# The weight and input streams of a convolutional feed-forward block are issued in another order, and the last block ends in two column halves

## The chip, the cores and the metric

One NeuronCore of a Trainium2 chip runs the whole program. The metric is the device time of one execution in microseconds. The kernel before takes 2106.96 us (median of 3 runs, 2106.72 to 2106.99).

## The reference, cut to what matters

One layer of a hybrid decoder trunk on 2048 positions and 1024 channels, float32. All of the work around the change is in the second half of the layer:

```python
x = x + concat([hm, hp]) @ w_out                 # output projection, residual
h = rmsnorm(x, g_ffn)
up = causal_dwconv(h @ w_up, w_ffn_conv) + b_ffn_conv   # 2 x 2816 channels, width 3
gate, val = up[..., :D_FF], up[..., D_FF:]
x = x + (silu(gate) * val) @ w_down
return rmsnorm(x, final_norm)
```

## The kernel before

Every float32 product is made of three matmuls. An operand is split into a rounded high part (`split_h`, L94, a cast on ACT) and the low part that is left (`split_l`, L100, a subtraction on DVE), and `products` (L112 to L114) issues high x high, high x low and low x high into one PSUM bank.

Positions come in four blocks of 512 (`b`). After the mixer, `out_proj` (L908) multiplies by `w_out` and adds the residual; its evacuation (L948) adds a PSUM bank to an `xr` tile that SP has loaded, ACT stores the sum to DRAM (`x2d`) and squares it (L919), and DVE adds the squares up (`ss`, L925). A bank is free for the next group when its square has been added up.

The feed-forward part runs in the order up half 0, down 0, down 1, up half 1, down 2, down 3. An up half handles two blocks at once by a scheme with seven products instead of eight, for each of 22 column blocks `j` (`PRODUCTS`: 11, S1, S2, 12, S3, 22, S4, where S1 to S4 take sums and differences of input quarters and of weight quarters). One product group (`j`, `p`) is 12 matmuls of 512 columns. Groups that build on another's result in the same bank have to wait until ACT has copied that bank to an `r` tile (`copied`, L1296): S2 after 11, S3 after S2, 22 after S3. `up_order` says in which order the groups run.

The order of the work is written out by hand. The main program issues matmuls, and after every few of them calls `tick()`, which lets each side stream (a generator) issue its next step. `until` lets a stream skip ticks until a flag is set, and `need` ticks until it is. Each engine then runs its own instructions in the order in which they were issued. The side streams that matter here:

- `w_stream` (L1051): for each weight item, in one tick the sum or difference of quarters on DVE if the product wants one (`w_source`, L1033) and the rounding on ACT, in the next tick the low part on DVE. There are nine slots for finished items. `raw_load` (L1020) loads a unit of weights on SP's queue when the unit before the last is used up.
- `b_first` (L1106): the 28 inputs (7 products x 4 row blocks) of the first up half. `scaled` multiplies each of the 16 loaded tiles by a vector on ACT (L1098) and by the inverse root on GpSimd (L1099), one tile to a tick; the main part of `b_first`, one tick behind, subtracts where the product wants it (L1102) and rounds; the low part follows one tick later. It starts in the middle of the last `out_proj` (`at`, L1225), which first issues two weight loads of 1 MB on SP, then the `xr` loads.
- `activate` (L1258): convolution taps (L1266 on ACT, L1269 on DVE), Silu (L1276, ACT), product (L1278, DVE) and store of one column block.
- `last_scale` (L1250): the inverse root for the last block, from inside the first up half.
- `squares2` and `final` (L1398, L1418): squares of the down part's results, the final RMSNorm and the stores.

`down(b)` (L1357) runs two halves of four PSUM banks; each weight item is one row block of 128 by 512 columns. All four banks of a half finish together, at the last row block.

Of the kernel before, what the change touches and what calls it, by code (L numbers as in the profile page):

```python
# [6 lines left out]
F32 = mybir.dt.float32  # L7
# [76 lines left out]
def trunk(tc, x, xT, w_in, w_gate, w_pool, w_out, w_up, w_down, vecs, cst, out):  # L84
# [43 lines left out]
    with ExitStack() as ctx:  # L128
# [136 lines left out]
        def until(*flag):  # L265
            while flag not in flags:
                yield
# [711 lines left out]
        PRODUCTS = ("11", "S1", "S2", "12", "S3", "22", "S4")  # L979
        A11, S1, S2, A12, S3, A22, S4 = range(7)  # L980
        NS, NS1, NW, NW1, NX = 28, 14, 9, 6, 5
        HOLD = NS1 - 6
        SLOTS = [f"mixT{i}" for i in range(KT)] + [f"s{i}" for i in range(HOLD)] + [f"hT{i}" for i in range(6)] \
            + [f"s{HOLD + i}" for i in (2, 3, 0, 1, 4, 5)]
# [16 lines left out]
        for j in range(NJ):  # L1001
            if j + 1 < NJ:
                up_order += [(j + 1, A11), (j, A22), (j + 1, S1), (j, S4), (j + 1, S2), (j + 1, A12), (j + 1, S3)]
            else:
                up_order += [(j, A22), (j, S4)]
        items, raw_units, first_item = [], [], {}
        for part in ("u0", "d0", "d1", "u1", "d2", "d3"):
            first_item[part] = len(items)
            n = int(part[1])
            if part[0] == "u":  # L1010
                items += [("u", n, j, p) for j, p in up_order]
                raw_units += [("u", n, j) for j in range(NJ)]
            else:
                items += [("d", n, h, j) for h in range(2) for j in range(NJ)]
                raw_units += [("d", n, h, i) for h in range(2) for i in range(0, NJ, 4)]
# [16 lines left out]

        def w_source(it, raw):  # L1033

            if it[0] == "d":
# [4 lines left out]
            if p == S1:  # L1040
                src = state["s1"] = ff1.tile([P, 512], F32, tag="sum", name="sum")
                dve.tensor_tensor(out=src, in0=q[1][0], in1=q[1][1], op=ALU.add)  # L1042
                return src
            if p == S2:
                dve.tensor_tensor(out=q[1][0], in0=q[0][0], in1=q[1][0], op=ALU.subtract)
                dve.tensor_tensor(out=q[0][0], in0=state.pop("s1"), in1=q[0][0], op=ALU.subtract)
            elif p == S4:
                dve.tensor_tensor(out=q[0][1], in0=q[0][1], in1=q[0][0], op=ALU.subtract)
            return {A11: q[0][0], S2: q[0][0], A12: q[0][1], S3: q[1][0], A22: q[1][1], S4: q[0][1]}[p]

        def w_stream():  # L1051

            for n, it in enumerate(items):
                while n >= NW and n - NW not in w_used:
                    yield
                if n == NW1 - 1:
                    yield from until("rr")
                elif NW1 <= n < NW1 + 2:
                    yield from until("op", NB - 1)
                elif n == NW1 + 2:  # L1060
                    yield from until("ff2")
                u = ("u", *it[1:3]) if it[0] == "u" else ("d", *it[1:3], it[3] // 4 * 4)
                while u not in raw_tiles:
                    yield
                src = w_source(it, raw_tiles[u])
                w = w_slot(n)
                split_h(w[:, 0], src)
                yield
                split_l(w[:, 0], w[:, 1], src)
                ws[n] = w  # L1070
                del w, src
                flags.add(("w", n))
                if it[3] == S4 if it[0] == "u" else it[3] % 4 == 3 or it[3] == NJ - 1:
                    del raw_tiles[u]
                    raw_load(raw_at[u] + 2)

        def x_tile():
            return ff1.tile([P, 512], F32, tag="x", name="x", bufs=NX)
# [27 lines left out]
        def b_first():  # L1106
# [27 lines left out]
            load(1)  # L1134
            yield from wait(2)
            sides.add(scaled())
            for p in range(7):
                for kk in range(4):
                    if p < 4:
                        yield from until("x2", p, kk)  # L1140
                    if p == S1:
                        sub(x[0, kk], x[1, kk], x[0, kk])
                    elif p == S2:
                        sub(x[1, kk], x[2, kk], x[1, kk], pool)
                        sub(x[0, kk], x[2, kk], x[0, kk])
                    elif p == A22 and kk == 0:
                        for i in range(4):
                            sub(x[3, i], x[3, i], x.pop((0, i)))
                    i = {A11: 0, S1: 0, S2: 0, A12: 3, S3: 1, A22: 3, S4: 2}[p]
                    yield from b_put(0, p, kk, x.pop((i, kk)) if p > A12 else x[i, kk])  # L1150

        def b_prep(hh):

# [71 lines left out]
        def at(hf):  # L1225
            nonlocal ff1
            if hf == 0:
                need("pool", NB - 1)
                need("ho", NB - 1)
                ph1.release()  # L1230
                sm1.release()
                ff1 = tc.alloc_tile_pool(name="ff1", bufs=1, side="right", reuse_waits="tile")
                raw_load(0)
                raw_load(1)
                sides.add(s_stream())
                sides.add(w_stream())

# [20 lines left out]
        def activate(hh, j, pre):  # L1258

            if hh and j < 2:  # L1260
                yield from until("fin", 1)
            y = [q_tile(4 + 2 * gv + j % 2)[:, 0:HT] for gv in range(2)]
            for gv in range(2):
                ch = gv * NJ + j
# [12 lines left out]
            flags.add(("act", hh, j))  # L1277
            dve.tensor_tensor(out=y[0], in0=y[0], in1=y[1], op=ALU.mult)  # L1278
            yield from wait(2)
            sp.dma_start(act_d[hh][j], y[0].rearrange("p (a c) -> p a c", a=2))  # L1280
# [76 lines left out]
        def down(b):  # L1357
# [10 lines left out]
                flags.add(("acc", b))  # L1368
            sides.add(acc_load())
            for h in range(2):  # L1370
                o = []
                for _ in range(4):
                    o.append(nbank([P, BT]) if len(down_banks) % 6 in (2, 3) else big())
                    down_banks.append(0)
                for j in range(NJ):
# [3 lines left out]
                    for i in range(4):  # L1379
# [15 lines left out]
                        if i % 2:  # L1395
                            tick()

        def squares2(b, acc, k, x):  # L1398

            if k == 0:  # L1400
# [12 lines left out]
                give(slot)  # L1413
            flags.add(("sq", b, k))
            if k == KT - 1:
                sides.add(final(b, acc))

        def final(b, acc):  # L1418

            last = b == NB - 1  # L1420
# [4 lines left out]
            yield from spread_rsqrt(r, f(ones_r), [state.pop("ss")], (0, 1, 0, 1) if last else (8, 2, 0, 1))  # L1425
            flags.add(("summed", b))
            for k in range(KT):
                x, g = acc[k // 2][:, k % 2], vec[:, V_FIN + k:V_FIN + k + 1]
                if last and k in (1, 3, 5):
                    act.activation(x, x, AF.Copy, scale=g)  # L1430
                    pool.tensor_tensor(out=x, in0=x, in1=r, op=ALU.mult)
                else:
                    dve.scalar_tensor_tensor(out=x, in0=x, scalar=g, in1=r, op0=ALU.mult, op1=ALU.mult)  # L1433
                if k % 2:
                    sp.dma_start(out[k // 2][:, :, b * BT:(b + 1) * BT], acc[k // 2])
                if not last and k % 2:
                    yield
                yield
            flags.add(("fin", b))
# [63 lines left out]
```

## Time and profile before

| | |
|---|---|
| median of 3 runs | 2106.96 us |
| the profiled execution | 2107.88 us, its span 2106.2 us |
| TensorE busy, matmuls | 1997.9 us (95%), 8876 |
| VectorE (DVE) | 1449.0 us (69%) |
| ScalarE (ACT) | 1043.5 us (50%) |
| GpSimd (POOL) | 182.7 us (9%) |
| granted TensorE clock, mean | 0.977 |

Busy shares are means over the whole span. The stages differ: TensorE is busy all the time in the down parts, and the other engines leave it waiting in a few places between and inside the other stages.

### The profile page before, as it was taken

The numbers are of one execution on the slowest core, as the hardware profiler recorded it, in microseconds if no ns is written. First come the engines' busy times: TensorE is split into PE (matmuls) and PEld (weight loads), VectorE is DVE, ScalarE is ACT, GpSimd is POOL, SyncE is SP. The second block draws the span as 40 slices with busy tenths as digits, with TensorE's granted clock in tenths as the row PEclk, the third lists the DMA queues.
The fourth block names the chain that finished last, engine by engine and source line by source line (L and its number), as shares of the span: only waits on it lengthen the run. The fifth ranks groups of instructions, "written<-read, shape, count | busy, mean of one in ns | idle before, by whom it ended". The sixth has DMA issues, their size and how long they took to land. (4 is left out here: it accounts for less than half of the span.)

```text
span 2106.2 us, 24399 instructions
## 1 busy us (share of the span) xinstructions
PE 1997.9 (95%) x8876; PEld 1627.0 (77%) x8876; DVE 1449.0 (69%) x2320; ACT 1043.5 (50%) x1838; POOL 182.7 (9%) x263
## 2 busy tenths in 40 slices
PE   8999999998997599999998999989999999999996
PEld 6777877776885488788886888877888888788885
DVE  6587777776675677777778546577777777765433
ACT  5655655755644444545446444344444544544321
POOL 1003002011021400000000001120000000000000
PEclk9999999999999799999999999999999999999998
DMA  5433544442347112222224644432212221375431
GB/s 188 148 106 114 158 144 135 131 155 71 109 147 249 55 66 95 89 77 80 90 80 153 228 150 180 142 108 96 105 71 80 91 90 71 125 245 190 143 117 40
DMA packets 107384, 258.62 MB, mean 123 GB/s; under 512 B 9472, under 2 KB 14080, under 8 KB 107264
## 3 DMA queue, kind: packets, MB, share of 16 engines
q1 hardware_dynamic: 101936, 247.37, 34.6%
q10 hardware_dynamic: 5328, 9.70, 1.2%
q8 instruction: 69, 1.13, 0.2%
q14 instruction: 51, 0.42, 0.1%
HBM read 215.81 MB, written 41.22 MB: 122 GB/s over the span
## 5 line engine op out<-in xcount | busy, mean ns | idle before, releaser
L112 PE MATMUL big<-s,w 128*128 128x512 f32 x1540 | 609.5, 396 | 44.4 <-ACT r L1296 30.5
L113 PE MATMUL big<-s,w 128*128 128x512 f32 x1540 | 604.2, 392 | 0.0
L114 PE MATMUL big<-s,w 128*128 128x512 f32 x1540 | 603.9, 392 | 0.0
L100 DVE TENSOR_TENSOR w<-raw,w 128x512 fp32r<-128x512 f32 x440 | 305.5, 696 | 193.8 <-ACT w L94 193.3
L94 ACT CAST w<-raw 128x512 fp32r<-128x512 f32 x440 | 267.1, 617 | 328.0 <-PE big L114 105.4
L112 PEld LDWEIGHTS big<-s,w 128*128 128x128 f32 x1540 | 291.9, 190 | 117.9 <-ACT r L1296 41.7
L114 PEld LDWEIGHTS big<-s,w 128*128 128x128 f32 x1540 | 291.9, 190 | 61.8
L113 PEld LDWEIGHTS big<-s,w 128*128 128x128 f32 x1540 | 292.2, 190 | 59.7 <-issue 0.7
L1269 DVE SCALAR_TENSOR_TENSOR q<-q,vec 128x1024 f32<-128x1024 f32 x176 | 225.8, 1283 | 85.5 <-ACT q L1266 53.1
L112 PE MATMUL num<-s,w 128*128 128x512 f32 x396 | 154.5, 390 | 0.0
L113 PE MATMUL num<-s,w 128*128 128x512 f32 x396 | 154.1, 389 | 0.0
L114 PE MATMUL num<-s,w 128*128 128x512 f32 x396 | 154.1, 389 | 0.0
L112 PE MATMUL big<-hT,whl 128*128 128x512 f32 x320 | 131.7, 411 | 20.6 <-DVE ss L925 8.1
L100 DVE TENSOR_TENSOR s<-x,s 128x512 fp32r<-128x512 f32 x120 | 84.5, 711 | 75.3 <-ACT s L94 74.5
L100 DVE TENSOR_TENSOR whl<-wraw,whl 128x1024 fp32r<-128x1024 f32 x92 | 116.2, 1264 | 28.4 <-ACT whl L94 28.0
L113 PE MATMUL big<-hT,whl 128*128 128x512 f32 x320 | 129.1, 403 | 0.9 <-DVE hT L102 0.9
L114 PE MATMUL big<-hT,whl 128*128 128x512 f32 x320 | 128.9, 403 | 0.0
L94 ACT CAST s<-x 128x512 fp32r<-128x512 f32 x120 | 73.0, 619 | 106.8 <-PE big L114 49.1
L1266 ACT ACTIVATE q<-q,vec 128x1024 f32<-128x1024 f32 x88 | 108.9, 1238 | 33.6 <-DVE q L1315 33.4
L94 ACT CAST w<-sum 128x512 fp32r<-128x512 f32 x44 | 27.3, 621 | 190.8 <-DVE sum L1042 190.8
L112 PE MATMUL big<-whl,hT 128*128 128x512 f32 x256 | 105.6, 413 | 0.0
L113 PE MATMUL big<-whl,hT 128*128 128x512 f32 x256 | 103.0, 402 | 1.7 <-DVE whl L100 1.7
(254 smaller groups left out, 2980.2 us busy)
## 6 DMA issues: line engine op xcount, KB each, us to landing
raw<-in_w_up SPq DMA_DIRECT2D x44, 1024.0 KB, 4.9
raw<-in_w_down SPq DMA_DIRECT2D x40, 1024.0 KB, 5.1
wraw<-in_w_in SPq DMA_DIRECT2D x60, 512.0 KB, 3.3
act<-q SPq DMA_DIRECT2D x44, 512.0 KB, 2.6
x<-act SPq DMA_DIRECT2D x88, 256.0 KB, 4.5
wraw<-in_w_out SPq DMA_DIRECT2D x32, 512.0 KB, 3.4
xr<-in_xT SPq DMA_DIRECT2D x32, 256.0 KB, 4.2
x2d<-xr ACTq DMA_DIRECT2D x32, 256.0 KB, 2.8
```

Of the source, the lines that this page charges most:

```text
L94: act.copy(out=h, in_=src)
L100: dve.tensor_tensor(out=l, in0=src, in1=f(h), op=ALU.subtract)
L112: pe.matmul(o, lhsT=lh, rhs=rh, start=first and i == 0, stop=False, skip_group_check=on)
L113: pe.matmul(o, lhsT=lh, rhs=rl, start=False, stop=False, skip_group_check=on)
L114: pe.matmul(o, lhsT=ll, rhs=rh, start=False, stop=last and i == n - 1, skip_group_check=on)
L1266: act.activation(y[gv], pre[gv][:, 2:2 + HT], AF.Identity, scale=tap[2], bias=vec[:, V_FB + ch:V_FB + ch + 1])
L1269: dve.scalar_tensor_tensor(out=y[gv], in0=pre[gv][:, n:n + HT], scalar=tap[n], in1=y[gv], op0=ALU.mult, op1=ALU.add)
```

## The change

Five edits.

1. `b_first` waits five ticks after it has started `scaled`, so that scaling runs four to five tiles ahead of its use. The low part of an input is issued after the rounding of the next one, and the four subtractions for product 22 are issued one to an input. The second weight load moves from `at` into `scaled`, behind the eighth tile.
2. `w_stream` issues the sum of item n, the rounding of item n - 1 and the low part of item n - 2 in one tick.
3. The last eight groups of `up_order` are in another order: with j the last column block, (j-1, 22), (j-1, S4), (j, S2), (j, S1), (j, S3), (j, 12), (j, 22), (j, S4). Before, they were (j-1, 22), (j, S1), (j-1, S4), (j, S2), (j, 12), (j, S3), (j, 22), (j, S4).
4. `activate` skips a tick at the start, issues Silu after the second channel's taps rather than the first's, and the product a tick after that.
5. The second half of the last `down` runs one 128-column group of outputs after another (`down_last`), with weight items of four row blocks by 128 columns. The last group runs twice on 256 positions, and `final_part` ends each of these halves by itself.

```diff
+        tail = [(NJ - 2, A22), (NJ - 2, S4), (NJ - 1, S2), (NJ - 1, S1), (NJ - 1, S3), (NJ - 1, A12), (NJ - 1, A22), (NJ - 1, S4)]
+        up_order[-len(tail):] = tail
...
+        items += [("e", NB - 1, k, g) for k in range(KT // 2, KT) for g in range(len(GROUPS))]
+        raw_units += [("e", NB - 1, k, i) for k in range(KT // 2, KT) for i in range(2)]
...
+            elif u[0] == "e":
+                k, i = u[2:]
+                lo, hi = ((0, 12), (12, NJ))[i]
+                src = w_down[lo * P:hi * P, k * P:(k + 1) * P].rearrange("(j p) c -> p j c", p=P)
+                sp.dma_start(t.rearrange("p g k c -> p (g k) c")[:, 0:hi - lo], src)
...
         def w_stream():
-                src = w_source(it, raw_tiles[u])
-                w = w_slot(n)
-                split_h(w[:, 0], src)
-                yield
-                split_l(w[:, 0], w[:, 1], src)
...
+            for n in range(len(items) + 2):
+                if rounded:
+                    done(*rounded)
+                    rounded = None
+                if summed:
...
+                    split_h(w[:, 0, 0:src.shape[-1]], src)
+                    rounded = k, it, w, src
+                if n < len(items):
...
+                    summed = n, items[n], w_source(items[n], raw_tiles[u])
+                yield
...
         def scaled():
+                        if (i, kk) == (1, 3):
+                            raw_load(1)
...
             sides.add(scaled())
-            for p in range(7):
-                for kk in range(4):
+            yield from wait(5)
...
+            for n in range(28):
+                p, kk = divmod(n, 4)
...
+                elif p == A22:
+                    sub(x[3, kk], x[3, kk], x.pop((0, kk)))
...
+                yield from s_free(n)
+                t = op_slot(n)
+                split_h(t[:, 0], src)
+                if last:
+                    low(last)
+                last = n, src, t
+                yield
...
         def activate(hh, j, pre):
+            yield
...
-                if gv == 0:
+                if gv == 1:
                     act.activation(y[0], y[0], AF.Silu)
             flags.add(("act", hh, j))
+            yield
             dve.tensor_tensor(out=y[0], in0=y[0], in1=y[1], op=ALU.mult)
...
+        def down_last(acc, n):
+            for k in range(KT // 2, KT - 1):
+                o = big()
+                for lo, hi in GROUPS:
+                    for j in range(lo, hi):
+                        products(o, [(parts(w, slice((j - lo) * P, (j - lo + 1) * P)), parts(as_[b, j]))], first=j == 0, last=j == NJ - 1)
...
+                dve.tensor_tensor(out=x, in0=o, in1=x, op=ALU.add)
+                sides.add(squares2(b, acc, k, x))
...
+            for c in range(2):
+                cs = slice(c * BT // 2, (c + 1) * BT // 2)
+                o = big()[:, 0:BT // 2]
...
+                        products(o, [(parts(w, slice((j - lo) * P, (j - lo + 1) * P)), (s[:, 0, cs], s[:, 1, cs]))], first=j == 0, last=j == NJ - 1)
...
+                dve.tensor_tensor(out=x[:, cs], in0=o, in1=x[:, cs], op=ALU.add)
+                sides.add(final_part(acc, r, sq, cs, c))
+
+        def final_part(acc, r, sq, cs, c):
+            act.activation(sq, x, AF.Square)
+            if c == 0:
+                yield from wait(3)
+            pe.matmul(v, lhsT=f(ones_r), rhs=state["ss"][:, cs], start=True, stop=False)
+            pe.matmul(v, lhsT=f(ones_r), rhs=sq, start=False, stop=True)
...
+            for k in range(KT):
+                x = acc[k // 2][:, k % 2, cs]
+                if k in (1, 3, 5):
+                    pool.tensor_tensor(out=x, in0=x, in1=r, op=ALU.mult)
+                else:
+                    dve.scalar_tensor_tensor(out=x, in0=x, scalar=vec[:, V_FIN + k:V_FIN + k + 1], in1=r, op0=ALU.mult, op1=ALU.mult)
+                if k % 2:
+                    sp.dma_start(out[k // 2][:, :, at + cs.start:at + cs.stop], acc[k // 2][:, :, cs])
```

## Rows read from the trace of the kernel before

**Rows 1.** Stages: length, then busy us (instructions) per engine; clock, DMA share, GB/s.

```profile
649.00:665.00 16.00, 12.20 (x54) 9.75 (x52) 8.26 (x13) 5.41 (x9) 0.00 (x0) 0.97 0.97 350
665.00:717.00 52.00, 30.09 (x98) 22.88 (x99) 27.29 (x36) 23.74 (x40) 29.59 (x21) 0.73 0.35 120
717.00:740.00 23.00, 17.09 (x55) 13.37 (x54) 19.85 (x33) 14.04 (x26) 0.33 (x3) 0.74 0.27 92
740.00:1160.00 420.00, 409.11 (x1780) 332.90 (x1779) 324.30 (x418) 213.85 (x319) 20.32 (x84) 0.99 0.26 92
1160.00:1400.00 240.00, 240.00 (x1053) 198.22 (x1053) 137.65 (x194) 102.85 (x173) 26.64 (x21) 1.00 0.50 172
1400.00:1850.00 450.00, 436.16 (x1893) 357.09 (x1893) 348.86 (x454) 223.03 (x337) 8.52 (x43) 0.98 0.26 90
2086.00:2106.20 20.20, 1.79 (x4) 0.30 (x2) 12.20 (x14) 6.47 (x10) 5.11 (x3) 0.62 0.27 104
```

**Rows 2.** Timeline of TensorE: start, duration, instruction, idle before and its releaser.

```profile
665.05 0.77 PE L112 MATMUL big<-hT,whl 128*128 128x512 f32 x1 [3.85 <-ACT w L94]
...
673.99 0.64 PE L112 MATMUL big<-hT,whl 128*128 128x512 f32 x1 [3.48 <-DVE ss L925]
...
685.92 0.80 PE L112 MATMUL big<-hT,whl 128*128 128x512 f32 x1 [4.59 <-DVE ss L925]
...
716.33 0.80 PE L112 MATMUL big<-s,w 128*128 128x512 f32 x1 [13.79 <-DVE ss L925]
...
730.59 0.80 PE L112 MATMUL big<-s,w 128*128 128x512 f32 x1 [5.91 <-ACT r L1296]
...
735.77 0.40 PE L112 MATMUL num<-s,w 128*128 128x512 f32 x1
```

**Rows 3.** Timeline of VectorE, the projection's first evacuation after the loads.

```profile
658.33 0.69 DVE L948 TENSOR_TENSOR xr<-big,xr 128x512 f32<-128x512 f32 x1 [5.58 <-DMA xr<-in_xT]
```

**Rows 4.** Timelines of GpSimd and ScalarE, one multiplication and two successive roundings.

```profile
686.62 1.27 POOL L1099 TENSOR_TENSOR xh<-xh,rr 128x512 f32<-128x512 f32 x1 [2.08 <-ACT xh L1098]
...
695.63 0.62 ACT L94 CAST s<-xh 128x512 fp32r<-128x512 f32 x1 [2.36 <-DVE xh L1102]
...
699.21 0.62 ACT L94 CAST s<-xh 128x512 fp32r<-128x512 f32 x1 [2.33 <-DVE xh L1102]
```

**Rows 5.** Timelines of GpSimd and VectorE where both are dense, and just after.

```profile
1392.89 5.97 POOL L1099 TENSOR_TENSOR x<-x,rr 128x512 f32<-128x512 f32 x4 [13.79 <-DVE raw L1046]
...
1394.37 1.62 DVE L100 TENSOR_TENSOR w<-raw,w 128x512 fp32r<-128x512 f32 x1 [1.78 <-ACT w L94]
...
1399.33 0.68 DVE L100 TENSOR_TENSOR w<-raw,w 128x512 fp32r<-128x512 f32 x1
```

**Rows 6.** TensorE's waits (total, times, longest), and three of them in the timeline.

```profile
PE big L112 <- ACT r L1296: 30.5, 10, 6.2
...
1156.96 0.80 PE L112 MATMUL big<-s,w 128*128 128x512 f32 x1 [3.58 <-ACT r L1296]
...
1417.08 0.80 PE L112 MATMUL big<-s,w 128*128 128x512 f32 x1 [6.21 <-ACT r L1296]
...
1468.05 0.80 PE L112 MATMUL big<-s,w 128*128 128x512 f32 x1 [4.08 <-ACT r L1296]
```

**Rows 7.** Timeline of ScalarE, a weight rounding ahead of a copy.

```profile
1415.39 0.62 ACT L94 CAST w<-raw 128x512 fp32r<-128x512 f32 x1 [2.17 <-DVE raw L1046]
```

**Rows 8.** Timeline of TensorE, successive matmuls of 260 columns.

```profile
145.69 0.28 PE L112 MATMUL num<-va,kws 128*128 128x260 f32 x1
145.81 0.28 PE L113 MATMUL num<-va,kws 128*128 128x260 f32 x1
```

**Rows 9.** Groups by line: busy us, mean ns of one, idle before, releaser.

```profile
L763 DVE TENSOR_TENSOR tmp<-mm,dm 128x256 f32<-128x256 f32 x32 | 12.0, 416 | 3.5 <-PE mm L114 3.5
```

**Rows 10.** Timelines of TensorE and VectorE at the end.

```profile
2090.08 1.48 PE L163 MATMUL mm<-ss,ones_r 128*128 128x512 f32 x2 [3.77 <-DVE ss L1412]
...
2095.69 6.41 DVE L1433 SCALAR_TENSOR_TENSOR q<-q,vec,rn 128x512 f32<-128x512 f32 x5
```

More of the change, by code (lines that the diff above doesn't have):

```diff
@@ L1039, in w_source @@
             q = [[raw[:, g, 4 * h:4 * h + 4].rearrange("p k c -> p (k c)") for h in range(2)] for g in range(2)]
[L1040 to L1044, printed above, removed]
+            if p in (S1, S2):
+                src = state.pop("s1", None)
+                if src is None:
+                    src = state["s1"] = ff1.tile([P, 512], F32, tag="sum", name="sum")
+                    dve.tensor_tensor(out=src, in0=q[1][0], in1=q[1][1], op=ALU.add)
+                if p == S1:
+                    return src
                 dve.tensor_tensor(out=q[1][0], in0=q[0][0], in1=q[1][0], op=ALU.subtract)
-                dve.tensor_tensor(out=q[0][0], in0=state.pop("s1"), in1=q[0][0], op=ALU.subtract)
+                dve.tensor_tensor(out=q[0][0], in0=src, in1=q[0][0], op=ALU.subtract)
             elif p == S4:
@@ L1051, in w_stream, with done @@
         def w_stream():
-            for n, it in enumerate(items):
-                while n >= NW and n - NW not in w_used:
-                    yield
[L1056 to L1064, printed above, removed]
-                src = w_source(it, raw_tiles[u])
-                w = w_slot(n)
-                split_h(w[:, 0], src)
-                yield
-                split_l(w[:, 0], w[:, 1], src)
+            def done(n, it, w, src):
+                m = src.shape[-1]
+                split_l(w[:, 0, 0:m], w[:, 1, 0:m], src)
@@ L1136, in b_first, with low @@
             sides.add(scaled())
-            for p in range(7):
-                for kk in range(4):
[L1139 to L1150, printed above, removed]
+            yield from wait(5)
+            last = None
+            def low(last):
+                n, src, t = last
+                split_l(t[:, 0], t[:, 1], src)
+                bs[0, n // 4, n % 4] = t
+                flags.add(("b", 0, n // 4, n % 4))
+            for n in range(28):
+                p, kk = divmod(n, 4)
+                if p < 4:
+                    yield from until("x2", p, kk)
+                if p == S1:
+                    sub(x[0, kk], x[1, kk], x[0, kk])
+                elif p == S2:
+                    sub(x[1, kk], x[2, kk], x[1, kk], pool)
+                    sub(x[0, kk], x[2, kk], x[0, kk])
+                elif p == A22:
+                    sub(x[3, kk], x[3, kk], x.pop((0, kk)))
+                i = {A11: 0, S1: 0, S2: 0, A12: 3, S3: 1, A22: 3, S4: 2}[p]
+                src = x.pop((i, kk)) if p > A12 else x[i, kk]
+                if last and n >= KT + HOLD:
+                    low(last)
+                    last = None
+                yield from s_free(n)
+                t = op_slot(n)
+                split_h(t[:, 0], src)
+                if last:
+                    low(last)
+                last = n, src, t
+                del src, t
+                yield
+            low(last)
         def b_prep(hh):
@@ L1233, in at @@
                 raw_load(0)
-                raw_load(1)
                 sides.add(s_stream())
@@ L1370, in down @@
             for h in range(2):
+                if (b, h) == (NB - 1, 1):
+                    down_last(acc, n)
+                    break
                 o = []
@@ new lines, in final_part @@
+        def final_part(acc, r, sq, cs, c):
+            k = KT - 1
+            slot = yield from take("mm", 2)
+            v, y = [bank([P, BT])[:, 0:BT // 2] for _ in range(2)]
+            r, sq, x = r[:, cs], sq[:, cs], acc[k // 2][:, k % 2, cs]
+            act.activation(sq, x, AF.Square)
[3 more added lines that the diff above has]
+            pe.matmul(v, lhsT=f(ones_r), rhs=sq, start=False, stop=True)
+            dve.tensor_scalar(r, v, 1.0 / D, EPS, op0=ALU.mult, op1=ALU.add)
+            act.activation(y, v, AF.Ln, scale=1.0 / D, bias=eps)
+            act.activation(y, y, AF.Exp, scale=-0.5)
+            act.activation(v, y, AF.Square)
+            if c == 0:
+                yield from wait(2)
+            dve.scalar_tensor_tensor(out=r, in0=v, scalar=-0.5, in1=r, op0=ALU.mult, op1=ALU.mult)
+            dve.scalar_tensor_tensor(out=r, in0=r, scalar=1.5, in1=y, op0=ALU.add, op1=ALU.mult)
+            give(slot)
+            for k in range(KT):
[5 more added lines that the diff above has]
+                if k % 2:
+                    at = (NB - 1) * BT
+                    sp.dma_start(out[k // 2][:, :, at + cs.start:at + cs.stop], acc[k // 2][:, :, cs])
+                    if c == 0:
+                        yield
@@ L1415, in squares2 @@
             if k == KT - 1:
+                assert b < NB - 1
                 sides.add(final(b, acc))
         def final(b, acc):
-            last = b == NB - 1
             exp_ln_tables()
@@ L1424, in final @@
             r = ff2.tile([P, BT], F32, tag="rn", name="rn")
-            yield from spread_rsqrt(r, f(ones_r), [state.pop("ss")], (0, 1, 0, 1) if last else (8, 2, 0, 1))
+            yield from spread_rsqrt(r, f(ones_r), [state.pop("ss")], (8, 2, 0, 1))
             flags.add(("summed", b))
@@ L1428, in final @@
                 x, g = acc[k // 2][:, k % 2], vec[:, V_FIN + k:V_FIN + k + 1]
[L1429 to L1433, printed above, removed]
+                dve.scalar_tensor_tensor(out=x, in0=x, scalar=g, in1=r, op0=ALU.mult, op1=ALU.mult)
                 if k % 2:
                     sp.dma_start(out[k // 2][:, :, b * BT:(b + 1) * BT], acc[k // 2])
-                if not last and k % 2:
+                if k % 2:
                     yield
```

66 lines of the change are left out of this document (62 added, 4 removed).

## The prediction

> **What bounds the kernel now.** First I read the stages (busy time per engine, matmuls counted). From 1160 to 1400 us TensorE never idles and a matmul of 512 columns costs 240.00 / 1053 = 0.228 us [rows 1]. That is the floor; the change removes no matmul of the long stages, so it can win only where TensorE waits or runs at the lower clock level. Three places show that. (A) From 649 to 740, the end of the output projection and the start of the first up part: idle 3.8 + 21.9 + 5.9 = 31.6 us, and the 98 + 55 matmuls of the last two stretches take 47.2 us where 0.228 each would be 34.9, so 12.3 us are clock (granted 0.73 and 0.74 of full on the mean, so partly at the 1.2 GHz level, behind the gaps). Together 43.9. (B) The two up parts, 740 to 1160 and 1400 to 1850: idle 10.9 + 13.8, clock (409.1 - 405.7) + (436.2 - 431.4), together 32.9. (C) The end, 20.2 us in which TensorE does almost nothing.
>
> Then I read what ends each wait. In A it is the sum of squares (DVE `ss`, L925), which frees the projection's PSUM banks, and once the copy out of PSUM (ACT `r`, L1296) [rows 2]. The evacuations behind `ss` stand in DVE's queue in order. There the first one waited 5.6 us for its `xr` load, which had two 1 MB weight loads ahead of it [rows 3]. Later the queues run at the pace of the scaling: between two roundings of input elements lie 3.58 us, of which ACT waits 2.3 for a subtraction, while GpSimd idles 2.1 us between multiplications of 1.27 us because its next scaling on ACT stands behind that rounding [rows 4]. The loop is ACT scale, GpSimd multiply, DVE subtract, ACT round, one element at a time. DVE and GpSimd are each busy for only 35.6 and 29.6 of the 68 us up to 717, ACT 29.2 [rows 1].
>
> **A, first up part's inputs.** With scaling five steps ahead the loop no longer has to close within a step, and the work must fit the engines. TensorE's own bound to the matmul group at 735.8 (the first on `num` [rows 2]) is 54 + 98 matmuls up to 717 and 34 more of the first three groups of 12 (two were before 717), 186 x 0.228 = 42.4 us, so 691.4 at the earliest.
>
> GpSimd's bound: 16 multiplications and 4 subtractions. Moving the second weight load (1 MB, L1026) behind the eighth scaling takes 1.05 MB / 350 GB/s = 3.0 us from ahead of `xr` and of the `xh` loads [rows 1], and the weight sums no longer hold ACT for DVE; I let the first multiplication start at 661 instead of 665.7. Alone, 20 x 1.27 = 25 us. But DVE will now be dense beside it. Where both were dense, four multiplications took 5.97 us and DVE's operations with two SBUF inputs 1.62 instead of 0.68 [rows 5]; three such stand between 1394.37 and the next undisturbed one at 1399.33, 1.65 a pair. All 20 paired: 33 us, so 694, and with the last rounding and low part about 695.5. If each wholly waited for the other, a pair would be 1.27 + 0.68 = 1.95 and the 20 take 39 us.
>
> The Trainium skill (SBUF — State Buffer, section "SBUF: two separate sides") says that a GpSimd instruction and a DVE instruction with two SBUF inputs exclude each other for their whole length. The trace agrees in kind, but its pair of 1.65 undercuts the 1.95 of whole lengths; by the rule the stage would end 6 us later than by the row, and the gain in A be 6 us smaller.
>
> DVE: its 35.6 us of before, started at 655 (the `xr` landing minus 3), end at 691 without any contention, and about 10 of the waits of 1.0 us that rows 5 show do not fall beside PSUM reads: 701. TensorE's banks hang on this queue. I take 701 and add 4.5 us for in-order coupling of three engines that are all nearly full: 705.5 instead of 735.8, **a gain of 30**. Bounds: 691.4 and full speed after it (44), and 715 (20: GpSimd starting at 665.7, pairs at 1.95, and 10 us for the rest of the stage and coupling). Below nothing is excluded only by the sizes: no bound here comes near 736.
>
> Moved with it: the second weight load passes `rr` and sixteen input loads in SP's queue. Its first user is weight item 5, which waits for the sixteenth scaling anyway; 3 us of transfer issued at about 672 hide under that. If that cover goes, TensorE waits for the sixth matmul group, at most those 3 us. The four subtractions for A22 now go one to an element instead of four at once; same work, no cost. The up order's first groups are unchanged, so the copy `r` of the first group, 5.9 us late, is late next: it stands behind the last roundings, and is inside my 4.5.
>
> **B, weight stream and up parts.** The PE wait for the copy `r` totals 30.5 us in ten waits [rows 6]; 5.9 belong to A. The copy itself waits for nothing but its turn on ACT; ahead of it stands a weight rounding that waits for DVE's sum or difference of the same tick (2.17 us before the copy that ended the wait of 1417) [rows 7]. The change issues the sum one tick before the rounding and the low part one tick after, so the rounding finds its source a tick earlier (six matmuls, 1.37 us). No instruction is added; each weight item is complete one tick later, hidden by nine slots of 2.7 us each.
> - 1156.96, 3.58 us: last group order, A22 directly behind S3. The new tail puts A12 (12 matmuls, 2.7 us) between them: all goes.
> - 1417.08 and 1468.05, 6.21 and 4.08: half each, 5.1; DVE is itself late there.
> - the other six, 30.5 - 5.91 - 3.58 - 6.21 - 4.08 = 10.7: under half, 4.9, since ACT's chain for the last block's scale (L1250 on), which also stands ahead of a copy, is not touched.
> - clock, 8.1: six tenths, 4.9.
>
> Sum 18.5. Silu and the product (L1276, L1278) are issued a step or two later, and behind them the store L1280; readers of the stored rows come many ticks later, so that is free unless ACT's copies now meet them; I keep 3.5 us for new waits: **15**. Bounds 4 (only the tail's wait) and 29 (all but that chain's share).
>
> **C, the tail.** In the new form the last column group runs 22 x 3 matmuls twice at 256 columns. The nearest rows, 260 columns, start 0.12 apart [rows 8]: 66 x (2 x 0.12 - 0.228) = 0.8 us more. Three of the four last groups finish earlier, so after the last matmul only one half-width add, square, reduction, inverse root and eight products remain. A half-width DVE operation costs 0.416 [rows 9] against 0.68, a factor 0.61. Before: TensorE's long run ends at 2086; 5.6 us lie between the reduction at 2090.1 and the first product at 2095.7, the products take 6.41, and 4.1 are left to 2106.2 [rows 1, 10]. After: add and square 1.0, 5.6 x 0.61 = 3.4, products 3.9, and 3.2 for half the bytes (between 2.0 and 4.1): 11.5. The first half's chain is as long as the 7.9 us of matmuls beside it and about 1.5 us more, and DVE works it off first: 13.0. With the 0.8, 13.8 instead of 20.2: **6.4**. Bounds 3 (the first half wholly ahead) and 9.
>
> The last block's weights now come in columns of 128 (512-byte runs) where no row of before shows such weight loads. 1.44 MB a column group at 350 GB/s take 4.1 us of its 66 x 0.228 = 15; at a quarter of that rate 16.5, 1.5 us late a group, 6 in all, before the nine-slot lead. I take nothing, as the engines moved 350 GB/s beside TensorE's work.
>
> **Sum.** 30 + 15 + 6.4 = 51.4 us from a span of 2106.2; the profiled run was 2107.88, 0.9 above the median of 2106.96, so 2106.96 - 51.4 = 2055.5.
>
> **Rivals.**
> (1) The shared work of DVE and GpSimd binds A: in favour, rows 5 and a DVE busy half of the time even now; against, GpSimd's idle 2.1 us per step. A gives 15 (between its low bound and coupling like that of before), B 14, C 6: 2072.
> (2) The scaling moves but the banks do not come free: `xr` and `ss` still decide, since DVE's evacuation stands behind more low parts than before. A 6, B 6, C 4: 2091. Rows 2 speak for it (three of five waits name `ss`), rows 4 against (what held `ss` was the element loop).
> (3) Slower. The later low part, Silu and product put ACT's copy `r` behind DVE once for each of the 44 column blocks of the up parts, with the 2.17 us of rows 7 on the path: 95 us, B's gain gone, A and C kept: 2106.96 - 36.4 + 95 = 2166. It decides from 36.4 / 44 = 0.8 us a block. For it: one block is 84 matmuls, and DVE is busy 77% of it. Against: the copy has 2.7 us of other matmuls as slack, and the order takes a DVE wait off ACT.
>
> **How the numbers follow.** Forecast 0.71 (own range 2038 to 2069: A 22 to 38, B 8 to 22, C 4 to 8, not all at one end); (1) 0.18; (2) 0.06; (3) 0.05, of which 0.01 stops near zero because its wait is nearer 0.8 us a block. The range for 8 in 10 reaches from 2038 over (1): 2038 to 2083. Below about 0.2% a measurement of this kernel can't be told from no change; faster 0.95, within 0.01, slower 0.04.
>
> **What would show it.** A right: the first matmul on `num` of the up part before 712, GpSimd's multiplications 1.3 to 1.7 us apart with no wait for ACT of 2 us, the waits for `ss` under 8 us in all. B right: no wait at the two up parts' ends, those after the start of the second up part halved. C right: 12 to 15 us from the last 256-column matmul to the end. Wrong: new waits on `w` or on the copy `r` inside the up parts, or waits for `ss` that stay above 15 us.

## The result and the profile after

The changed kernel takes 2070.94 us (median of 4 runs, 2067.22 to 2072.59) against 2106.84 before: ratio 0.9825, 95% interval 0.9813 to 0.9836, 36 us faster. That lies in the range given (2038 to 2083), but 15 us above the forecast of 2055.5, 2 us above the forecast's own range (2038 to 2069) and next to rival (1), 2072. Its profiled execution took 2070.96 us with a span of 2069.2.

The stages of the changed kernel, columns as in [rows 1] (after the length, busy time and instructions of TensorE's matmuls, its weight loads, VectorE, ScalarE and GpSimd):

```profile
665.00:705.00 40.00, 21.81 (x84) 17.21 (x84) 35.00 (x32) 20.82 (x34) 28.50 (x21) 0.80 0.46 161
705.00:723.00 18.00, 13.29 (x37) 10.27 (x38) 17.97 (x31) 10.76 (x21) 0.00 (x0) 0.69 0.35 120
723.00:1145.00 422.00, 417.88 (x1826) 344.47 (x1826) 328.00 (x423) 220.82 (x328) 19.07 (x84) 0.99 0.28 90
...
1378.00:1830.00 452.00, 442.92 (x1940) 364.95 (x1939) 356.69 (x465) 231.92 (x347) 57.23 (x44) 0.99 0.29 95
2056.70:2069.20 12.50, 1.17 (x5) 0.36 (x3) 6.38 (x11) 1.60 (x4) 2.99 (x4) 0.69 0.50 168
```

VectorE (third pair) is now busy for 35.0 of 40 us and then for 17.97 of 18: the stage that waited for a loop is now full on one engine. TensorE's idle time in the two up parts (third and fourth row) is 4.1 + 9.1 us, where [rows 1] show 10.9 + 13.8; the end is 12.5 us.

The timeline of TensorE in the changed kernel; the first line is a wait that all these kernels have just ahead of the change, and serves below as the mark from which stages are counted, the last but three the first matmul on `num`:

```profile
635.56 0.49 PE L112 MATMUL num<-prs,wp 128*128 128x512 f32 x1 [1.00 <-ACT prs L94]
...
670.90 0.79 PE L112 MATMUL big<-hT,whl 128*128 128x512 f32 x1 [6.93 <-DVE ss L925]
...
705.34 0.80 PE L112 MATMUL big<-s,w 128*128 128x512 f32 x1 [12.15 <-DVE ss L925]
...
717.49 0.80 PE L112 MATMUL big<-s,w 128*128 128x512 f32 x1 [4.37 <-ACT r L1359]
...
722.77 0.63 PE L112 MATMUL num<-s,w 128*128 128x512 f32 x1
...
864.51 0.79 PE L112 MATMUL big<-s,w 128*128 128x512 f32 x1 [4.12 <-ACT r L1359]
...
1395.34 0.80 PE L112 MATMUL big<-s,w 128*128 128x512 f32 x1 [7.07 <-ACT r L1359]
...
1443.85 0.50 PE L112 MATMUL big<-s,w 128*128 128x512 f32 x1 [2.02 <-ACT r L1359]
```

The same mark in the kernel before:

```profile
636.76 0.50 PE L112 MATMUL num<-prs,wp 128*128 128x512 f32 x1 [1.00 <-ACT prs L94]
```

Counted from the mark, the first matmul on `num` comes at 99.0 us before (735.77 in [rows 2]) and at 87.2 after. The bank that the up part's first group needs comes free at 79.6 us before (716.33 in [rows 2]) and at 69.8 after (705.34). So 9.8 of the 11.8 us are this bank, and 2.0 the three groups of matmuls between it and `num`.

The part ahead of the mark has the same instructions in all kernels, and still its end moved between 635.6 and 640.2 over the profiled runs; so the lengths below are counted from the mark. They scatter too: four kernels (the changed one, `u3_old_order`, `u4_old_silu` and `m5_squares_later`) have the same instructions up to the first matmul on `num`, and it comes at 85.7 to 87.9 in them. A difference of about 2 us or less between two profiled runs shows nothing by itself.

Where the 37 us of span went: 1.2 ahead of the mark, 11.8 in A, 17.0 in B (11.5 of idle time, 5.5 of clock), 6.9 in C (20.2 less 12.5, less the 0.8 that the prediction puts on the narrower matmuls).

Why A gave 12 and not 30 begins in these lines. First VectorE's evacuations and GpSimd's multiplications:

```profile
655.20 0.69 DVE L948 TENSOR_TENSOR xr<-big,xr 128x512 f32<-128x512 f32 x1 [3.43 <-DMA xr<-in_xT]
...
667.81 0.69 DVE L948 TENSOR_TENSOR xr<-big,xr 128x512 f32<-128x512 f32 x1 [4.15 <-DMA xr<-in_xT]
```

```profile
661.35 3.44 POOL L1139 TENSOR_TENSOR xh<-xh,rr 128x512 f32<-128x512 f32 x2 [54.61 <-ACT xh L1138]
670.22 2.52 POOL L1139 TENSOR_TENSOR xh<-xh,rr 128x512 f32<-128x512 f32 x2 [5.44 <-ACT xh L1138]
```

The first evacuation comes 3.1 us earlier and the multiplications start at 661.35, both as forecast. But the third evacuation waits again for its load, and two multiplications after the start GpSimd waits 5.4 us, because the next scaling stands in ACT's queue behind the store (`x2d`) of that evacuation and a rounding:

```profile
668.54 0.33 ACTq L949 DMA_DIRECT2D x2d<-xr  x1
668.90 0.62 ACT L94 CAST w<-raw 128x512 fp32r<-128x512 f32 x1 [5.98 <-DVE xr L948]
```

SP's queue shows why the load is late: it is issued behind the eight input loads.

```profile
651.36 10.20 SPq L1160 DMA_DIRECT2D xh<-x2d  x8
661.66 0.40 SPq L226 DMA_DIRECT2D wraw<-in_w_out  x1
662.10 0.91 SPq L937 DMA_DIRECT2D xr<-in_xT  x2
```

Then VectorE and GpSimd, where both are dense:

```profile
687.78 1.78 DVE L100 TENSOR_TENSOR s<-xh,s 128x512 fp32r<-128x512 f32 x1
689.49 1.77 DVE L1142 TENSOR_TENSOR xh<-x,xh 128x512 f32<-128x512 f32 x1
691.18 1.78 DVE L100 TENSOR_TENSOR s<-xh,s 128x512 fp32r<-128x512 f32 x1
...
704.61 0.68 DVE L925 TENSOR_TENSOR ss<-big,ss 128x512 f32<-128x512 f32 x1
```

```profile
690.67 1.75 POOL L1142 TENSOR_TENSOR xh<-x,xh 128x512 f32<-128x512 f32 x1
692.62 1.48 POOL L1139 TENSOR_TENSOR xh<-xh,rr 128x512 f32<-128x512 f32 x1 [0.20 <-ACT xh L1138]
```

One of each takes 1.70 us, near the 1.65 that [rows 5] gave. The Trainium skill (SBUF — State Buffer, section "SBUF: two separate sides") says that a GpSimd instruction and a VectorE instruction with two SBUF inputs exclude each other for the whole instruction. The alternation agrees; the 1.70 does not quite, as the two lengths alone make 1.95. The last VectorE line, at 704.61, is what TensorE waits for at 705.34: the add that frees the bank of the up part's first group stands in that queue.

### The profile page after: what moved, and what is told of

Same layout as the page of the kernel before. It is cut to its first block, busy times and chain, and to the rows that moved or that the text cites. A ratio compares the mean times of both kernels' runs of the same rounds, so it can differ in the third digit from the quotient of the medians.

```text
span 2069.2 us, 24627 instructions
## 1 busy us (share of the span) xinstructions
PE 1986.1 (96%) x8948; PEld 1628.5 (79%) x8948; DVE 1457.3 (70%) x2330; ACT 1047.1 (51%) x1844; POOL 236.5 (11%) x266
## 4 chain that ended last, share of the span: by engine, by line
PE 77%; DVE 11%; ACT 5%; DMA 4%; issue 2%; SPq 1%; DVEq 0%; POOL 0%; ACTq 0%; POOLq 0%
PE big L112 21%; PE big L113 21%; PE big L114 21%; PE num L114 4%; PE num L113 4%; PE num L112 4%; DVE whl L100 1%; DVE s L100 1%; ACT hjunk L819 1%; DMA x<-x2d 1%; DVE tmp L519 1%; PE mm L503 1%; DVE w L100 1%; DVE hT L102 1%; ACT whl L94 1%
## 5 line engine op out<-in xcount | busy, mean ns | idle before, releaser
L112 PE MATMUL big<-s,w 128*128 128x512 f32 (+1 forms) x1562 | 609.3, 390 | 29.7 <-ACT r L1359 17.6
L114 PE MATMUL big<-s,w 128*128 128x512 f32 (+1 forms) x1562 | 606.7, 388 | 0.0
L113 PE MATMUL big<-s,w 128*128 128x512 f32 (+1 forms) x1562 | 606.5, 388 | 0.0
L94 ACT CAST w<-raw 128x512 fp32r<-128x512 f32 (+1 forms) x442 | 272.7, 619 | 502.8 <-PE big L114 378.1
L100 DVE TENSOR_TENSOR w<-raw,w 128x512 fp32r<-128x512 f32 (+1 forms) x442 | 306.2, 695 | 219.6 <-ACT w L94 214.5
L112 PEld LDWEIGHTS big<-s,w 128*128 128x128 f32 x1562 | 295.6, 189 | 94.3 <-ACT r L1359 19.6
L114 PEld LDWEIGHTS big<-s,w 128*128 128x128 f32 x1562 | 295.4, 189 | 60.5
L113 PEld LDWEIGHTS big<-s,w 128*128 128x128 f32 x1562 | 295.7, 189 | 59.4 <-issue 0.7
L1352 POOL COPY q<-halo 128x2 f32<-128x2 f32 x88 | 64.4, 749 | 362.5 <-DVE q L1331 295.8
```

The lines of the kernel that those rows point to most:

```text
L94: act.copy(out=h, in_=src)
L100: dve.tensor_tensor(out=l, in0=src, in1=f(h), op=ALU.subtract)
L112: pe.matmul(o, lhsT=lh, rhs=rh, start=first and i == 0, stop=False, skip_group_check=on)
L113: pe.matmul(o, lhsT=lh, rhs=rl, start=False, stop=False, skip_group_check=on)
L114: pe.matmul(o, lhsT=ll, rhs=rh, start=False, stop=last and i == n - 1, skip_group_check=on)
L1352: pool.tensor_copy(t[:, 0:2], halo[:, gv * NJ + j])
```

## The experiments

Each is the changed kernel with the edit shown (`m3`, `m4`, `m7` build on others). Ratios are against the kernel before, timed along with each. "First num" and "end" are counted from the mark in the profiled run.

| kernel | ratio, 95% interval | first num | end |
|---|---|---|---|
| before | 1 | 99.0 | 1469.4 |
| changed | 0.9825 (0.9813 to 0.9836) | 87.2 | 1433.6 |
| u1_old_first | 0.9860 (0.9844 to 0.9876) | 95.5 | 1440.5 |
| m1_xr_ahead | 0.9817 (0.9802 to 0.9831) | 83.0 | 1431.4 |
| m2_no_gpsimd | 0.9801 (0.9787 to 0.9816) | 81.9 | 1426.3 |
| m3_both | 0.9783 (0.9769 to 0.9798) | 78.4 | 1423.9 |
| m4_sum_sooner | 0.9799 (0.9784 to 0.9814) | 77.8 | 1427.1 |
| u2_old_stream | 0.9852 (0.9837 to 0.9868) | 87.5 | 1436.5 |
| u3_old_order | 0.9870 (0.9845 to 0.9894) | 86.1 | 1435.8 |
| u4_old_silu | 0.9815 (0.9801 to 0.9830) | 85.7 | 1429.8 |
| u5_old_stream_silu | 0.9879 (0.9864 to 0.9894) | 88.0 | 1442.9 |
| u6_first_and_tail_only | 0.9932 (0.9915 to 0.9949) | 88.5 | 1452.3 |
| m5_squares_later | 0.9867 (0.9851 to 0.9883) | 87.9 | 1441.8 |
| m7_sum_sooner_old_silu | 0.9778 (0.9764 to 0.9793) | 78.7 | 1420.9 |

**The first part undone.** `b_first` and the second weight load as before.

> The changed kernel with the first up part's inputs as before (scaling one step ahead, second weight load early); everything else changed. Theory: the trace of the changed kernel puts the first matmul on num of the up part 12 us earlier than before, counted from the same matmul at 637 us, so undoing it costs 12: 2083 us. Rival, the prediction's own size of this part: 30 us, 2101.

0.9860, 7 us slower than the changed kernel; the first matmul on `num` comes 8.3 us later. So the first part's own edit is worth 8. The other 3.5 of A's 11.8 appear with the old first part in place. Of the other edits only the weight stream's order runs ahead of that matmul (`activate` starts behind a later group), and beside the new first part the kernels with the old stream (`u2`, `u5`, `u6`) come only 0.3 to 1.3 us later than the changed one, inside the scatter. What makes up the 3.5 is not shown.

**The xr loads.**

```diff
-                        sp.dma_start(xr[k], xT[b, k])
+                        (act if b == NB - 1 and k in (2, 3) else sp).dma_start(xr[k], xT[b, k])
```

> The changed kernel, with the third and fourth xr loads of the last output projection issued on ACT's DMA queue, not on SP's behind the eight xh loads. Theory (loads in order): VectorE's wait of 4.2 us for xr at 667.8 goes, with it GpSimd's gap of 5.4 and TensorE's wait of 6.9 at 670.9; the scaling starts its run 5 us earlier, 5 to 9 us faster, about 2064. Rival (VectorE and GpSimd share a port and bind alone): the first wait goes, but the later one for ss (12.2) grows by as much, 2069 to 2071.

TensorE's waits in this kernel:

```profile
670.14 0.80 PE L112 MATMUL big<-hT,whl 128*128 128x512 f32 x1 [3.69 <-DVE ss L925]
...
704.70 0.79 PE L112 MATMUL big<-s,w 128*128 128x512 f32 x1 [12.17 <-DVE ss L925]
...
721.18 0.40 PE L112 MATMUL num<-s,w 128*128 128x512 f32 x1
```

VectorE no longer waits for the third load, the wait of 6.9 falls to 3.7, and the stage is 4.2 us shorter; the later wait of 12.2 has not grown. In the time as measured that is 0.0008, inside the intervals, so the 4 us stand on the traces alone. The rival's time came true, its mechanism did not: the later wait did not take up what the first one lost. The expected 5 to 9 us are not reached.

**No GpSimd in the first part.** One VectorE operation does both factors of the scaling, and the four subtractions move to VectorE.

```diff
-                        b_scale(x[i, kk], kk + 4 * kh, rr[0][:, a])
+                        k = kk + 4 * kh
+                        dve.scalar_tensor_tensor(out=x[i, kk], in0=x[i, kk], scalar=vec[:, V_FFN + k:V_FFN + k + 1], in1=rr[0][:, a], op0=ALU.mult, op1=ALU.mult)
...
-                    sub(x[1, kk], x[2, kk], x[1, kk], pool)
+                    sub(x[1, kk], x[2, kk], x[1, kk])
```

> The changed kernel, with scaling and all subtractions of the first up part's inputs on VectorE (one operation does both factors, so ACT's 16 scalings go too), GpSimd idle there. Theory (GpSimd and VectorE take turns at a port, 1.67 us a pair): VectorE's operations fall back from 1.7 to 0.68 us, 20 more of 0.7 to 0.85 come to it, about 16 us against the 20 pairs' extra 1.0 each, so 0 to 8 us faster, 2063 to 2071. Rival (the two run side by side, and the 1.7 us are slow operations for another reason): VectorE has 16 us more to do in a stage it fills, 2080 or more. Third (the round trip ACT, GpSimd, VectorE is what binds): it is gone, 15 us faster or more, 2055.

```profile
702.26 0.80 PE L112 MATMUL big<-s,w 128*128 128x512 f32 x1 [8.15 <-DVE ss L925]
```

The stage is 5.3 us shorter, TensorE's wait falls from 12.15 to 8.15, and the ratio is 0.0024 lower, with intervals that touch. Putting 20 more operations on the engine that already binds made it faster: that is what turn-taking predicts, and the reverse of what two engines side by side would do. The round trip from ACT to GpSimd to VectorE was not what bound (15 us or more were not gained). The edit takes 16 scalings from ACT as well, so how much of the 5.3 us is turn-taking alone is not separated; that VectorE's operations are short again without GpSimd is seen in the next kernel.

> Both edits of the two kernels before it: xr loads 3 and 4 on ACT's queue, and no GpSimd in the first part. Theory: the two causes add, since the first sets when the run starts and the second how long it takes: 8 to 15 us faster, 2056 to 2063. Rival (either one alone brings all there is): no better than the better of the two by over 2 us.

VectorE in `m3_both`, and TensorE:

```profile
692.79 0.68 DVE L100 TENSOR_TENSOR s<-xh,s 128x512 fp32r<-128x512 f32 x1
693.39 0.74 DVE L1168 SCALAR_TENSOR_TENSOR xh<-xh,vec,rr 128x512 f32<-128x512 f32 x1
694.05 1.28 DVE L1142 TENSOR_TENSOR xh<-x,xh 128x512 f32<-128x512 f32 x2
...
697.73 0.68 DVE L925 TENSOR_TENSOR ss<-big,ss 128x512 f32<-128x512 f32 x1
```

```profile
698.46 0.80 PE L112 MATMUL big<-s,w 128*128 128x512 f32 x1 [8.05 <-DVE ss L925]
...
715.50 0.40 PE L112 MATMUL num<-s,w 128*128 128x512 f32 x1
```

The operations are back at 0.68, where they took 1.75 to 1.78 beside GpSimd, and the two edits nearly add: 4.2 and 5.3 alone, 8.8 together. VectorE has no gap left from 668 to 712; what remains is its amount of work.

**The sum sooner.** On `m3_both`:

```diff
-                yield from wait(2)
+                yield from wait(1 if b == NB - 1 else 2)
```

> m3_both, with the sum of squares that frees a projection bank issued one tick after its square, not two, for the last block. Theory (the bank for the up part's first group is held by where this add stands in VectorE's full queue): TensorE's wait for ss before the first up matmul, 8.1 us in m3_both, falls to 4 to 6, and the wait of 4.1 at 669 shrinks too: 2 to 5 us faster than m3_both's ratio of 0.9783, 0.976 to 0.9775. Rival (VectorE's amount of work binds, not its order): the later wait for the copy r (5.0) grows by what this one loses, 0.978 to 0.979.

```profile
697.56 0.79 PE L112 MATMUL big<-s,w 128*128 128x512 f32 x1 [7.29 <-DVE ss L925]
...
709.50 0.50 PE L112 MATMUL big<-s,w 128*128 128x512 f32 x1 [3.48 <-ACT r L1360]
```

The wait fell by 0.8 and the stage by 0.6, inside the scatter, and the time is no better than that of `m3_both`. The theory of the order fell; the rival (the amount of work binds) fits, though the wait for the copy `r` fell from 5.0 to 3.5 and did not grow as it said.

**The up parts, one edit undone at a time.**

> The changed kernel with the weight stream's timing as before: sum and rounding of an item in one tick, low part in the next. Theory (roundings no longer wait for the sum of their own tick): the small waits for the copy r inside the up parts come back, the up parts' idle time rises from 13 to about 20 us with some clock, and the first part loses the 3 us that it had over its own edit: 6 to 12 us slower than the changed kernel's ratio of 0.9825, 0.985 to 0.988. Rival (Silu's later issue did it): within 2 us, 0.982 to 0.9835.

> The changed kernel with the up parts' last eight groups in the order of before. Theory: product 22 stands directly behind S3 again, at both up parts' ends, so waits of 3 to 4 us at each end, one with 2.5 us at the low clock: 5 to 9 us slower, ratio 0.985 to 0.987. Rival (the spaced weight stream alone lets the copy come in time): under 2 us, 0.982 to 0.9835.

> The changed kernel with activate as before (Silu after the first channel's taps, no skipped ticks). Theory (ACT stands still ahead of Silu while VectorE does the taps, 1 to 2 us per column block, and the copy r behind it is late only where VectorE is late too): 0 to 5 us slower, ratio 0.9825 to 0.985. Rival (the later Silu is what cost the prediction's 3.5 us of new waits): 1 to 4 us faster, 0.981 to 0.982.

TensorE in `u3_old_order`:

```profile
1132.60 0.50 PE L112 MATMUL big<-s,w 128*128 128x512 f32 x1 [0.66 <-ACT r L1358]
...
1138.37 0.50 PE L112 MATMUL big<-s,w 128*128 128x512 f32 x1 [2.74 <-ACT r L1358]
...
1811.27 0.50 PE L112 MATMUL big<-s,w 128*128 128x512 f32 x1 [1.19 <-ACT r L1358]
```

With the old order the waits at both ends are back, 4.6 us, without the low clock. The ratio rose by 0.0045, with a wide interval (2073 to 2085 us); the profiled run is the fastest of the four and only 2.2 us longer from the mark, so the size of this cost stays open. With the old stream the time rose by 0.0027 as expected, but not for the reason given: inside the up parts its waits are those of the changed kernel (4.13, 8.29 and 2.02 against 4.12, 7.07 and 2.02), the small ones do not come back. Where its time goes is not shown. With the old Silu the kernel is no slower; the profiled span is 3.8 us shorter from the mark, the ratio 0.0010 lower, which the intervals do not separate from nothing.

**Two undone together.**

> The changed kernel with both the weight stream's timing and activate as before (new: first part, group order at the ends, tail). Undone one at a time they cost +2.9 and -3.9 us in the profiled spans, counted from the same matmul at 636 us. Theory (either of the two takes the same ACT wait off the copy r): undone together they cost far more than the sum, 7 to 12 us, ratio 0.986 to 0.988, and the small waits inside the up parts are back. Rival (the group order at the ends did it all): the sum of the two, about the changed kernel's 0.9825, within 0.0015.

Two small waits of the kernel before, and the waits of this one:

```profile
1135.20 0.50 PE L112 MATMUL big<-s,w 128*128 128x512 f32 x1 [1.87 <-ACT r L1296]
...
1822.09 0.50 PE L112 MATMUL big<-s,w 128*128 128x512 f32 x1 [1.85 <-ACT r L1296]
```

```profile
866.01 0.50 PE L112 MATMUL big<-s,w 128*128 128x512 f32 x1 [3.41 <-ACT r L1346]
...
1123.92 0.50 PE L112 MATMUL big<-s,w 128*128 128x512 f32 x1 [1.66 <-ACT r L1346]
...
1449.52 0.80 PE L112 MATMUL big<-s,w 128*128 128x512 f32 x1 [4.08 <-ACT r L1346]
...
1802.86 0.50 PE L112 MATMUL big<-s,w 128*128 128x512 f32 x1 [1.68 <-ACT r L1346]
```

Now these waits are back one by one: 1.66 and 1.68 for those of 1.87 and 1.85 before, and 4.08 as in [rows 6], where the old stream alone leaves 2.02 and the old Silu alone 1.62. The cost is 0.0054 where the two alone made 0.0017 (from the mark 9.3 us where they made -0.9). For these waits either edit is enough to let the copy `r` come in time.

> Weight stream, activate and group order all as before; new are only the first part's inputs and the tail. Theory: what the traces put on the up parts, 17 us, is lost: ratio 0.9825 + 0.0081 = 0.9906, between 0.989 and 0.992. Rival (the up parts' gain is partly the first part's, whose shift changes what meets what): ratio under 0.988.

0.9932, so the three up-part edits together are worth 0.0107, 22 us (18.7 from the mark, 1.3 of them ahead of `num`): somewhat more than the 17 read from the traces, and not a by-product of the first part. TensorE's waits for the copy `r` behind the first `num` add up to 25.1 us here and to 24.5 before; in the changed kernel they are 13.2.

**The squares ahead of the second up part.** `squares2` waits six ticks at k = 4 of the second down part.

```diff
             else:
+                if b == 1 and k == 4:
+                    yield from wait(6)
                 yield from until("sq", b, k - 1)
```

> The changed kernel, with the squares of the second down part's last half (four on ACT, each waiting for VectorE's add of the one before) begun six ticks later. Theory: the copy r at the start of the second up part stands behind them on ACT (idle 2.8 and 0.7 us there for VectorE's sums), so TensorE's wait of 7.1 us at 1395 falls to 3 or less and the clock stays up: 4 to 7 us faster, ratio 0.979 to 0.981. Rival (VectorE's backlog alone holds the copy's weight rounding): the wait changes by under 1.5 us, 0.982 to 0.983.

```profile
1397.94 0.79 PE L112 MATMUL big<-s,w 128*128 128x512 f32 x1 [5.21 <-ACT r L1359]
...
1472.71 0.80 PE L112 MATMUL big<-s,w 128*128 128x512 f32 x1 [5.72 <-ACT r L1359]
```

ACT, ahead of the copies that end these two waits:

```profile
1396.78 0.62 ACT L94 CAST w<-raw 128x512 fp32r<-128x512 f32 x1 [4.38 <-DVE raw L1065]
...
1470.95 1.24 ACT L1328 ACTIVATE q<-q,vec 128x1024 f32<-128x1024 f32 x1 [6.01 <-DMA act<-q]
```

The wait fell by 1.9, not by 4 or more. With the squares out of the way a weight rounding stands ahead of the copy and waits 4.4 us for VectorE's difference: VectorE's backlog holds this rounding, as the rival had it, though no run took that backlog away. And the delayed squares delayed the final norm, for whose end the first two `activate` streams wait. These two now run together, and the next one's first tap on ACT waits 6.0 us for a store (`act<-q`) that frees its tile. The copy behind it is late: a new wait of 5.7 us appeared at 1472, and the kernel is slower than the changed one.

**A faster version.** `m4_sum_sooner` with the old `activate`:

> m4_sum_sooner with activate as before, the two edits that the runs so far favour put together. Theory (they act in different stages and add): 2 to 4 us faster than m4_sum_sooner, ratio 0.974 to 0.9765. Rival (the gain of the old activate was a difference between runs): equal to m4_sum_sooner within 0.001.

2059.46 us (median), ratio 0.9778 (0.9764 to 0.9793): its interval lies below that of the changed kernel, so it beats both. Against `m4_sum_sooner` it is 0.0021 lower, in the expected direction, with intervals that overlap; against `m3_both` (0.9783) it is the same. So what is shown to beat the changed kernel are the two edits of `m3_both`; the other two add nothing that these runs can tell.

## Why the prediction came out as it did

**A, the mis-sized term: 30 forecast, 11.8 measured, below the low bound of 20.** The inputs to the sum held: first evacuation at 655, first multiplication at 661, a pair at 1.65 (1.70), VectorE busy for 45.2 us from 649 to the bank (35.6 and 10 in the sum). Even its result held: "TensorE's banks hang on this queue. I take 701 and add 4.5 us" gave 705.5, and at 705.34 the bank came free. The step that failed is the next one, "705.5 instead of 735.8": it sets the freeing of the bank against the first matmul on `num`. The bank of before came free at 716.33 [rows 2]; against that, 705.5 is a gain of 11, and 9.8 were measured.
- The three groups before `num` follow only behind the bank. They took 17.4 us (19.4 before): 36 x 0.228 = 8.2, the 4.4 of the copy `r`, and 4.8 because both waits left the clock at the lower level for matmuls behind them, which start 0.43 us apart (mean granted clock 0.69). I had let these groups run beside the end of VectorE's queue. But the 35.6 us of VectorE's work that I counted end at 717; 17.0 more stood between there and `num` before, and in the changed kernel VectorE is busy for 17.40 of these 17.43 us. The 17.4 us are all but about 1 us of the 18 that are missing.
- GpSimd ended at 704, not at 694: I moved the first `xr` load forward and did not look at the third, in the same in-order queue behind eight loads. `m1_xr_ahead` prices that at 4.2 us. It did not add to the error only by luck: VectorE's wait of 4.2 for this load used up the 4.5 that I had allowed for coupling.

The signs for A failed: the first matmul on `num` was not before 712 (722.77), GpSimd waited for ACT by more than 2 us (5.44), and the waits for `ss` were 19.1 us, neither under 8 nor under the 15 above which the prediction was to count as wrong here.

Rival (1) named the shared work of VectorE and GpSimd. It bears on A, but it is not the step that failed: ending the sharing (`m2_no_gpsimd`) gives 5.3 us, and the forecast had priced a pair about right. That its 2072 came within about 1 us is partly luck: it had A 15, B 14 and C 6, where 11.8, 17.0, 6.9 and 1.2 ahead of the mark were measured. Rival (2) named the wait that decided, the one for the banks, with gains that were too small. The time lies in the wide range only because that was drawn over rival (1); the forecast's own range for A began at 22.

**B, 15 forecast, 17.0 measured in the traces.** Right: the wait of 1156.96 gone and, in `u3_old_order`, back in part (2.74 for 3.58); the wait of 1468.05 halved (2.02); the chain at 877 untouched (4.12 in one wait, 3.38 and 0.76 before). Wrong in detail: the wait of 1417.08 did not halve (7.07 for 6.21), the other six gave 6.6 and not 4.9, and the reserve of 3.5 for new waits was not needed; these errors cancel in part. The reason given, that a rounding finds its source a tick earlier, is only half shown: undone alone it brings no wait back, because the later Silu, which I had counted only as a risk, does the same.

**C, 6.4 forecast, 6.9 measured.** The last halves of TensorE and VectorE in the changed kernel:

```profile
2040.01 0.28 PE L113 MATMUL big<-s,w 128*128 128x256 f32 x1
2040.13 0.28 PE L114 MATMUL big<-s,w 128*128 128x256 f32 x1
```

```profile
2057.84 0.41 DVE L1505 TENSOR_TENSOR q<-big,q 128x256 f32<-128x256 f32 x1
...
2062.14 3.57 DVE L1534 SCALAR_TENSOR_TENSOR q<-q,vec,rn 128x256 f32<-128x256 f32 x5
```

Matmuls 0.12 apart, products 3.57 (3.9 forecast), and the second half's add 1.1 us after its matmuls end (1.5 forecast), behind the first half's products. The narrow weight loads made no wait. No run undoes the tail alone; in `u6_first_and_tail_only`, 17.1 us shorter than before from the mark, 10.5 lie ahead of `num`, and the 6.6 that are left fit.

The sum came out 15 us too high: 18 in A, against which B, C and the 1.2 us ahead of the mark came out 4 better. Nothing speaks for rival (3).

## What to carry to other kernels

When a wait is to go, find the instruction that ends it and count what stands ahead of that instruction in its engine's queue after the change. Set its new time against its own old time, not against a later instruction: the work that the wait held back starts only then, here with its first matmuls at the lower clock. Follow every load that the stage needs through the in-order DMA queue, not only the first. And undo edits together as well as singly: two that each remove the same wait look worthless one at a time.

## What had not been expected of the hardware

GpSimd's small copies ahead of each column block (two columns each) took 220 ns on the mean before and 749 in the changed kernel, 64.4 us instead of 19.1 in all; first the kernel before, then the changed one:

```profile
L1289 POOL COPY q<-halo 128x2 f32<-128x2 f32 x88 | 19.1, 220 | 413.9 <-DVE q L1269 413.9
...
L1352 POOL COPY q<-halo 128x2 f32<-128x2 f32 x88 | 64.4, 749 | 362.5 <-DVE q L1331 295.8 <-ACT q L1328 66.7
```

The growth is all in the second up part, where 44 of them take 57.6 us (9.7 before); the 44 of the first part take 6.8 (9.4 before). No wait of another engine names them in the changed kernel, so they cost nothing that the profile shows. Why they grew was not tested.
